# Right factors of the gated MLP in the projection's stream tiles, four of seven made inside the out projection; whole residual rows in two buffers; the first chunk's loads on ScalarE's queue

## The chip, the cores and the metric

One core of a Trainium2 chip runs the whole program in one launch. The metric is the device time in microseconds (us), the median of three runs. Engines are named as the profile names them: PE is TensorE's matmul and PEld its weight load, DVE is VectorE, ACT is ScalarE, POOL is GpSimd, SP is SyncE. A "q" behind a name (SPq, ACTq) is that engine's queue of transfers.

## What is computed

A trunk of two layers, one step for 1032 columns (1024 of a prompt, 8 of samples). Each layer has a mixer, then a gated MLP with a short convolution, both behind an RMSNorm and added to the stream:

```python
def _rmsnorm(x, g):
    y = xf * lax.rsqrt(jnp.mean(xf * xf, axis=-1, keepdims=True) + EPS)
    return (y * g.astype(jnp.float32)).astype(x.dtype)

def _conv_ffn(xn, w_up, conv_w, conv_b, w_down, conv_state):
    gpre, up = jnp.split(xn @ w_up, 2, axis=-1)
    full = jnp.concatenate([conv_state.astype(gpre.dtype), gpre], axis=1)
    acc = conv_b + full[:, 0:t] * conv_w[0]
    ...
    h = jax.nn.gelu(acc) * up
    return h @ w_down, full[:, full.shape[1] - (CONV_W - 1):]
...
        d, s_, c_, k_, w_ = _even_mixer(_rmsnorm(xs, norm_mix[l]), ...)   # ends in mixed @ w_out
        xs = xs + d
        ...
        d, cv = _conv_ffn(_rmsnorm(xs, norm_ffn[l]), *fp, state_ffn_conv[l])
        xs = xs + d
```

The model width is 1024 (8 blocks of 128 rows), the MLP's inner width 2816 (22 blocks, `NF`).

## The kernel before, in words

**Arithmetic.** Data lies transposed: 128 rows of a block on the partitions, TT = 1032 columns. A float32 product is made of three TensorE passes over a high and a low part of each operand: ACT writes the high part, DVE subtracts it from the value to get the low part. The stream of a layer is held as eight pairs `xh[m]`, `xl[m]`.

**Out projection** (`out_project`, L376 to L421). Eight output blocks m in the order `PAIRS` = 0, 4, 1, 5, 2, 6, 3, 7. Behind each block's matmuls (L285) POOL adds the block's high and low stream parts (L412), DVE adds the product (L416), ACT writes the new row times its gain to `big[:, m]` (L417), SP stores the row to `res` in DRAM (L418), ACT squares it (L419) and `add_sq` adds the squares up (L205).

**Climb** (`climb`, the up projection). The 1024 x 256 piece of the weight for one inner block f and the eight rows of `big` are cut into 2 x 2, and `seven` (L514) multiplies them by seven products instead of eight, in three PSUM banks in the order "abcabcb". A product has 24 matmuls of 258 columns (L534), 3 passes x 4 blocks x 2 halves. Its left factor comes from `factors` (L447): two loads of 512 KB into `wr` and `wr2` (L452), two sums on POOL (L456, L457), a split by ACT and DVE per product (L464, L466, L467). `fill` keeps four left factors ahead. Its right factor is four tiles (`slot`) of [128, 2, 2, 260]. There are 28 slots; they are made once, in f = 0, by `first` (L750), at the time when the product that needs them is issued: sums of `big` quarters (`sums`, L436 to L440) on POOL and DVE, then `parts`, a copy on ACT (L444) and a subtraction on DVE (L445). The pools of the out projection and of the stream tiles are closed by then, and the MLP's pools lie in their place. The inner blocks' results are turned into right factors of the next product and stored to `hid` in DRAM by SP (L718, L721, L722), through two staging tiles.

**Descend** (`descend`, the down projection). Pairs of inner blocks in chunks of two pairs, the last chunk of three; for each chunk four units j = 0 to 3, each of seven products of 12 matmuls (18 in the last chunk). Right factors come back from `hid` by `load_factors` (L602 to L607), the first chunk's on SP while the climb's last block still runs, later ones on ACT's queue. DVE (L810) adds each product to quarters of `big`. In chunks 1 and 2, behind product 6 of each unit, the residual of two half rows is loaded on SP (L826), multiplied by `std` (L827) and added to `big` (L828) on POOL; the halves share one tile `sq_t`.

**Layer 1's end.** Four inner blocks are left over. Behind the last chunk their rows `raw` are loaded (L584), split (`split_o`, L373, L374), and `finish` (L887) multiplies them by eight pieces of weight, which `last_weight` loads and splits (L260, L273, L274), then norms and transposes the output. At the end of layer 0, L595 and L596 split `big` into the stream tiles of layer 1.

**What sets the order.** Each engine runs its instructions in the order in which the program was written in the MLP (`ordered`); outside it a scheduler orders them. `plan(step, late, ...)` puts a piece of work behind the product with that number.

Of the kernel before, what the change touches and what calls it, by code (L numbers as in the profile page):

```python
# [9 lines left out]
F32 = mybir.dt.float32  # L10
# [61 lines left out]
class Trunk:  # L72
# [22 lines left out]
    def setup(self):  # L95
# [14 lines left out]
        self.order, self.rung = range(KD), 0  # L110
        self.open_x()
# [3 lines left out]
    def open_x(self):  # L115

        self.xp = self.tp(name="xp", bufs=1, side="right")
        pool = self.xp.__enter__()
        self.xh, self.xl = [None] * KD, [None] * KD
        for k in PAIRS[::-1]:  # L120
            self.xh[k], self.xl[k] = (pool.tile([128, TT], F32R, name=f"{x}{k}") for x in ("xh", "xl"))
# [255 lines left out]
    def out_project(self, l, w, split, ks, ready, late, nat=None):  # L377
# [3 lines left out]
        with self.tp(name="opp", bufs=2, space=PSUM) as pp, \  # L381
# [25 lines left out]
            self.res = self.dram.tile([KD, 128, TT], F32, name="res")  # L407
            for n, m in enumerate(PAIRS):
# [22 lines left out]
    def sums(self, i, b, eng):  # L431
# [9 lines left out]
        return self.halves((b11, b11, b21, b12, b11, b21, b22)[i])  # L441

# [105 lines left out]
    def ffn(self, l, last):  # L548
        nc, a, tc, big = self.nc, self.a, self.tc, self.big
        w_up, w_dn = a["ffn_w_up"][l], a["ffn_w_down"][l]  # L550
        pools = [self.tp(name="fr", bufs=1, side="right"), self.tp(name="fx", bufs=1, side="right"),
                 self.tp(name="fl", bufs=1)]
        self.fr, self.fx, self.fl = (p.__enter__() for p in pools)
        right = [self.slot(i) for i in range(8)] + [None] * 20
        for i in range(27, 7, -1):
            right[i] = self.slot(i)
        NP = 9 if last else 11
        hid = self.dram.tile([NP, 7, 128, 2, 2, QW + 2], F32, name="hid")
# [7 lines left out]
        self.st = self.fx.tile([128, 2, 2, QW + 2], F32R, name="st")  # L566
# [11 lines left out]
        pools.pop().__exit__(None, None, None)  # L578
        if last:
            with self.tp(name="fin", bufs=1) as fin:  # L580
                y = [fin.tile([128, TT], F32, name=f"y{i}") for i in range(4)]
                parts = []
                for k in range(4):
                    nc.sync.dma_start(y[k], raw[k])  # L584
                    parts.append(self.split_o(fin, k, y[k]))
                wts = [self.last_weight(w_dn[18 * 128:], 4, m, fin) for m in range(KD)]
                with self.tp(name="flp", bufs=8, space=PSUM) as self.ps:
                    self.finish(wts, [p[0] for p in parts], [p[1] for p in parts], y)
        while pools:
            pools.pop().__exit__(None, None, None)  # L590
        if not last:
# [1713 lines left out]
```

## Time and profile before

| | |
|---|---|
| median of three runs | 2974.23 us (2973.86 to 2976.27) |
| profiled execution | 2967.24 us; span of its records 2965.5 us |
| PE busy | 2753.7 us, 93% of the span |
| DVE, ACT, POOL busy | 61%, 45%, 38% |
| DMA, mean | 116 GB/s |
| mean granted TensorE clock | 0.96 of full speed |

The page also cuts the span into 40 equal slices of 74.1 us. Busy shares and the clock are in tenths:

```profile
PE   8999999999996999998878999999969999999798
...
PEclk9999999999897999999989999999979999999899
DMA  6620001531131344347755212221212344467522
```

A row of a timeline merges neighbours of one kind ("x22" is 22 instructions), and ends with the idle time of the engine ahead of it and what ended it. A row of the chain of waits is a piece of the path that ends last. Some matmul records are missing from the trace, so counts in the rows can be short of the program's.

### The profile page before, as it was taken

Reading aid. Unit: us, or ns where it says so; the run is one execution under the profiler, and the core shown is the slowest. Engines: PE = TensorE matmul, PEld = TensorE weight load, DVE = VectorE, ACT = ScalarE, POOL = GpSimd, SP = SyncE. Lnnn points to the kernel's source line nnn. Section 1 sums busy time; section 2 is a strip of 40 time slices with the busy share of each in tenths; the row PEclk is TensorE's granted clock in tenths of the full one; section 3 lists DMA queues with packets and bytes.
Section 4 is the critical chain, followed back from the end, with each engine's and each line's share of the span. In section 5 each row is a group of like instructions: output and inputs, shape, how many; then the busy total and the mean of one; then the engine's idle time right before and its main releaser. Section 6 shows DMA issues by size and latency. Waiting matters only on the chain.

```text
span 2965.5 us, 49527 instructions
## 1 busy us (share of the span) xinstructions
PE 2753.7 (93%) x19507; PEld 2496.5 (84%) x19507; DVE 1819.4 (61%) x3060; ACT 1334.1 (45%) x2543; POOL 1126.0 (38%) x1088
## 2 busy tenths in 40 slices
PE   8999999999996999998878999999969999999798
PEld 7885445887895999998878989888959999999698
DVE  6566765466626787776445754445356778765456
ACT  4343443334434666655434422324345666655234
POOL 3621234321153545553445411110344554554633
PEclk9999999999897999999989999999979999999899
DMA  6620001531131344347755212221212344467522
GB/s 182 187 63 29 36 1 56 192 108 37 42 96 31 103 151 157 138 139 271 247 172 200 55 36 66 63 63 45 89 50 65 139 149 151 142 224 260 194 83 108
DMA packets 300652, 342.67 MB, mean 116 GB/s; under 512 B 33997, under 2 KB 246068, under 8 KB 300356
## 3 DMA queue, kind: packets, MB, share of 16 engines
q1 hardware_dynamic: 269692, 238.97, 24.8%
q10 hardware_dynamic: 21000, 66.98, 6.2%
q0 software_dynamic: 9728, 33.56, 3.3%
q8 instruction: 154, 2.52, 0.4%
q14 instruction: 78, 0.64, 0.1%
HBM read 241.13 MB, written 102.50 MB: 116 GB/s over the span
## 4 chain that ended last, share of the span: by engine, by line
PE 78%; DVE 8%; POOL 4%; DMA 4%; ACT 3%; issue 2%; ACTq 0%; DVEq 0%; SPq 0%; POOLq 0%
PE ppb L534 16%; PE ps L285 13%; PE ppc L534 11%; PE ppa L534 10%; PE pp L285 6%; PE ps L1410 2%; PE pd L285 2%; DMA sq_t<-res 2%; PE ps L887 2%; PE pd L1319 1%; POOL big L828 1%; PE ps L1167 1%; PE pd L1385 1%; PE ps L1155 1%; PE pd L1386 1%
## 5 line engine op out<-in xcount | busy, mean ns | idle before, releaser
L534 PE MATMUL ppb<-s,wh 128*128 128x258 f32 x2376 | 315.8, 288 | 16.0 <-DVE s L445 5.3
L534 PE MATMUL ppb<-s,wl 128*128 128x258 f32 x2376 | 313.7, 287 | 9.6 <-ACT s L444 3.5
L534 PEld LDWEIGHTS ppb<-s,wh 128*128 128x128 f32 x2376 | 303.3, 196 | 18.2 <-ACT ps L466 6.2
L534 PEld LDWEIGHTS ppb<-s,wl 128*128 128x128 f32 x2376 | 300.4, 194 | 12.1 <-ACT s L444 4.1
L467 DVE TENSOR_TENSOR wh<-ps,wh 128x512 fp32r<-128x512 f32 (+2 forms) x280 | 162.4, 580 | 181.9 <-ACT ps L466 179.6
L534 PE MATMUL ppc<-s,wh 128*128 128x258 f32 x1536 | 211.5, 295 | 48.1 <-DVE big L810 22.8
L534 PE MATMUL ppc<-s,wl 128*128 128x258 f32 x1536 | 209.2, 292 | 47.5 <-DVE big L810 27.5
L534 PEld LDWEIGHTS ppc<-s,wh 128*128 128x128 f32 x1536 | 202.8, 202 | 50.2 <-ACT ps L466 18.0
L534 PEld LDWEIGHTS ppc<-s,wl 128*128 128x128 f32 x1536 | 199.6, 198 | 51.3 <-ACT wl L464 21.6
L467 DVE TENSOR_TENSOR wl<-ps,wl 128x512 fp32r<-128x512 f32 (+2 forms) x280 | 161.9, 578 | 131.0 <-ACT ps L466 129.3
L285 PE MATMUL ps<-xh,wh 128*128 128x344 f32 x960 | 223.7, 338 | 0.0
L285 PE MATMUL ps<-xl,wh 128*128 128x344 f32 x960 | 215.4, 328 | 5.1 <-DVE xl L596 2.7
L534 PE MATMUL ppa<-s,wl 128*128 128x258 f32 x1536 | 204.4, 287 | 14.1 <-ACT s L444 8.1
L272 POOL TENSOR_TENSOR wr<-wr,gains 128x1024 f32<-128x1024 f32 (+1 forms) x44 | 83.6, 1899 | 338.7 <-DMA wr<-in_odd_w_in_dram 217.0
L285 PE MATMUL ps<-xh,wl 128*128 128x344 f32 x960 | 210.6, 325 | 0.0
L534 PEld LDWEIGHTS ppa<-s,wl 128*128 128x128 f32 x1536 | 194.4, 194 | 17.0 <-ACT s L444 8.6
L534 PE MATMUL ppa<-s,wh 128*128 128x258 f32 x1536 | 200.8, 285 | 8.2 <-ACT tu L808 8.2
L534 PEld LDWEIGHTS ppa<-s,wh 128*128 128x128 f32 x1536 | 192.9, 192 | 8.9 <-ACT tu L808 8.4
L466 ACT COPY ps<-wr 128x512 f32<-128x512 f32 (+2 forms) x400 | 198.5, 496 | 2.8 <-DVE st L734 1.8
L464 ACT ACTIVATE wh<-wr 128x512 fp32r<-128x512 f32 (+2 forms) x200 | 108.6, 543 | 176.2 <-PE ppb L534 69.5
L464 ACT ACTIVATE wl<-wr 128x512 fp32r<-128x512 f32 (+2 forms) x200 | 108.6, 543 | 170.6 <-PE ppb L534 60.0
L472 POOL TENSOR_TENSOR wr<-wr,wr 128x512 f32<-128x512 f32 (+2 forms) x80 | 94.3, 1179 | 230.3 <-ACT ps L466 230.2
(780 smaller groups left out, 6064.4 us busy)
## 6 DMA issues: line engine op xcount, KB each, us to landing
s<-hid ACTq DMA_DIRECT2D x112, 520.0 KB
wr<-in_ffn_w_up_dram SPq DMA_DIRECT2D x88, 512.0 KB
hid<-big SPq DMA_DIRECT2D x67, 520.0 KB
hid<-st SPq DMA_DIRECT2D x66, 520.0 KB
wr<-in_ffn_w_down_dram SPq DMA_DIRECT2D x64, 256.0 KB
s<-hid SPq DMA_DIRECT2D x28, 520.0 KB
wr<-in_odd_w_in_dram SPq DMA_DIRECT2D x24, 512.0 KB
wr<-in_even_w_in_dram SPq DMA_DIRECT2D x18, 512.0 KB
```

Source lines behind the costliest of these rows:

```text
L272: self.gain_eng.tensor_tensor(raw, raw, gain[:, :, None].to_broadcast([128, kt, m]), op=OP.mult)
L285: nc.tensor.matmul(outs[g], l[:, kw, :], r[k][:, g * GW:(g + 1) * GW], start=(n == 0 and i == 0), stop=(n == kt - 1 and i == 2))
L464: nc.scalar.activation(hi, x, AF.Copy)
L466: nc.scalar.copy(pt, x)
L467: nc.vector.tensor_tensor(lo, pt, hi, op=OP.subtract)
L472: nc.gpsimd.tensor_tensor(a11, a11, a21, op=OP.subtract)
L534: nc.tensor.matmul(pt[:, q], w[:, k], r[:, part, q, :QW], start=(new and k == 0 and n == 0), stop=(k == len(right) - 1 and n == 2), skip_g ...
L828: p.tensor_tensor(big[:, m, s], big[:, m, s], x, op=OP.add)
L887: nc.tensor.matmul(pt, l[:, k, :], r[k][:, s], start=(k == 0 and i == 0), stop=(k == n - 1 and i == 2))
L1155: nc.tensor.transpose(pt[:, j * 128:(j + 1) * 128], kv[:, half * 4 + j, sl * 256 + c * 128:sl * 256 + c * 128 + 128], self.ident)
L1167: nc.tensor.matmul(hid[c][64 * h:64 * h + 64, :273], wt[:, c, q], xt[h][:, q, :273], start=(g == 0 and q == 0), stop=(g == 7 and q == 3))
L1410: nc.tensor.matmul(po[64 * g:64 * g + 64], v[:, kb, 64 * g:64 * g + 64], p[:, g * 512:(g + 1) * 512], start=first, stop=last)
```

## The change

1. The pool of the stream tiles stays open through the MLP. The 16 tiles `xh0` to `xl7` are slots 0 to 15; slots 16 to 27 are new tiles as before. A slot is [128, 2, 2, 258] now, so rows of `hid` have 4128 bytes instead of 4160, and the two zero fills of the pad are gone.
2. `prepare(j)` makes the right factors 0, 1, 2 and 4 of the column of blocks j, j + 4 (they are the ones that products 0 to 3 take) inside the out projection, behind every second block. All `sums` of `big` are on DVE. The twelve tiles of products 4 to 6 are planned three at a time behind products 0 to 3 of f = 0.
3. A residual row is loaded whole one unit ahead, at product 0, into `sq_t` or `sq` in turn; POOL multiplies at product 2 and adds at product 6. In layer 1 the eight rows are taken two units earlier.
4. The first chunk's loads are issued on ACT's queue.
5. At the end of layer 1 the four `raw` rows are loaded into free stream tiles, and the eight pieces of weight are loaded and split from m = 7 down to m = 0.
6. Layer 1's stream tiles come from the open pool.

```diff
+        self.pools.append(self.tp(name="xp", bufs=1, side="right"))
+        self.xp = self.pools[-1].__enter__()
         self.open_x()
...
+            self.right = [None] * 28
             for n, m in enumerate(PAIRS):
...
                 self.add_sq(x, n)
-        self.xp.__exit__(None, None, None)
+                if n % 2:
+                    self.prepare(n // 2)
...
     def slot(self, i):
-        return (self.fl if i > 7 else self.fr).tile([128, 2, 2, QW + 2], F32R, name=f"s{i}")
+        if i < 16:
+            return self.xp.tile([128, 2, 2, QW], F32R, name=("xh", "xl")[i // 4 % 2] + str(i % 4 + i // 8 * 4))
+        return self.fl.tile([128, 2, 2, QW], F32R, name=f"s{i}")
...
+    def quads(self, j):
+        return [self.big[:, m, s] for m in (j, j + 4) for s in (slice(0, HW), slice(HW, TT))]
+
+    def first_right(self, n, j):
+        i = 4 * MADE[n] + j
+        if i < 16:
+            self.right[i] = self.slot(i)
+        self.parts(self.right[i], self.halves(self.quads(j)[(0, 0, 2, 1, 0, 2, 3)[n]]))
+
+    def prepare(self, j):
+        for n in (0, 1, 2, 4):
+            self.sums(n, self.quads(j), self.nc.vector)
+            self.first_right(n, j)
...
-        pools = [self.tp(name="fr", bufs=1, side="right"), self.tp(name="fx", bufs=1, side="right"),
-                 self.tp(name="fl", bufs=1)]
+        pools = [self.tp(name="fx", bufs=1, side="right"), self.tp(name="fl", bufs=1)]
...
-                y = [fin.tile([128, TT], F32, name=f"y{i}") for i in range(4)]
-                parts = []
+                free = [self.slot(i).rearrange("p a q w -> p (a q w)") for i in (1, 3, 5, 7, 9, 11, 13)]
+                wts = [self.last_weight(w_dn[18 * 128:], 4, m, fin) for m in range(KD)[::-1]][::-1]
+                y, parts = [x.bitcast(F32) for x in free[:4]], free[4:]
+                while len(parts) < 8:
+                    parts.insert(3, fin.tile([128, TT], F32R, name=f"o{len(parts)}"))
                 for k in range(4):
                     nc.sync.dma_start(y[k], raw[k])
-                    parts.append(self.split_o(fin, k, y[k]))
-                wts = [self.last_weight(w_dn[18 * 128:], 4, m, fin) for m in range(KD)]
+                    nc.scalar.activation(parts[k], y[k], AF.Copy)
+                    nc.vector.tensor_tensor(parts[4 + k], y[k], parts[k], op=OP.subtract)
...
-        def first(i):
-            for n in ((0,), (1,), (2, 4), (3,), (), (6,), (5,))[i]:
-                for j in range(4):
-                    self.sums(n, xs[j], p if j < (2 if n == 1 else 3) else v)
-                for j in range(4):
-                    self.parts(right[4 * MADE[n] + j], self.halves(xs[j][(0, 0, 2, 1, 0, 2, 3)[n]]))
-            return right[4 * i:4 * i + 4]
+        for k in range(12):
+            self.plan(k // 3, 1, lambda k=k: self.first_right((3, 6, 5)[k // 4], k % 4))
...
-                        self.load_factors(c, n, hid, range(2 * i, min(2 * i + 2, 7)), nc.sync)
+                        self.load_factors(c, n, hid, range(2 * i, min(2 * i + 2, 7)), nc.scalar)
...
-                    for n in {1: (0, 1), 2: (2, 3)}.get(c, ()) if i == 6 else ():
-                        m, s = j + n // 2 * 4, slice(n % 2 * HW, n % 2 * HW + HW)
-                        x = self.vec.tile([128, TT], F32, name="sq_t")[:, s]
-                        nc.sync.dma_start(x, self.res[m][:, s])
-                        p.tensor_tensor(x, x, self.std[:, s], op=OP.mult)
-                        p.tensor_tensor(big[:, m, s], big[:, m, s], x, op=OP.add)
+                    r = 4 * c + j - (2 if last else 4)
+                    if i == 0 and -1 <= r < 7:
+                        rows[r + 1] = self.vec.tile([128, TT], F32, name=("sq_t", "sq")[r % 2])
+                        nc.sync.dma_start(rows[r + 1], self.res[r + 1])
+                    if i == 2 and 0 <= r < 8:
+                        p.tensor_tensor(rows[r], rows[r], self.std, op=OP.mult)
+                    if i == 6 and 0 <= r < 8:
+                        p.tensor_tensor(big[:, r], big[:, r], rows[r], op=OP.add)
```

**First place: SP's queue at the end of layer 0's out projection.** Before, the last stores of `res` and the MLP's first weight loads (`wr_7969` is the second half of f = 0's weights, a `wr2` tile):

```order
L418 DMA res<-rstd 128x1032
L452 DMA wr<-in_ffn_w_up_dram 128x8x128
L452 DMA wr_7969<-in_ffn_w_up_dram 128x8x128
L452 DMA wr_7977<-in_ffn_w_up_dram 128x8x128
L418 DMA res<-sq_t 128x1032
L418 DMA res<-rstd 128x1032
```

Now (`wr_8013` is that tile):

```order
L419 DMA res<-rstd 128x1032
L473 DMA wr<-in_ffn_w_up_dram 128x8x128
L419 DMA res<-sq_t 128x1032
L473 DMA wr_8013<-in_ffn_w_up_dram 128x8x128
L419 DMA res<-rstd 128x1032
L473 DMA wr_8021<-in_ffn_w_up_dram 128x8x128
```

The load of the second half went from ahead of the two last stores to between them. The pool `fx`, where it lands, now lies over the out projection's operands `oh` and `ol`, and the load waits for the last matmul of the out projection that reads them.

**Second place: POOL in the second chunk of layer 0, one unit.** Before, four residual operations on half rows (L827, L828) stand together between two operations of the left factors (L472, L476):

```order
L456 TENSOR_TENSOR s_14310<-wr_14205 128x256
L457 TENSOR_TENSOR s_14311<-s_14310,wr 128x256
L472 TENSOR_TENSOR wr<-wr,wr_14205 128x2x128
L827 TENSOR_TENSOR sq_t<-sq_t,std 128x516
L828 TENSOR_TENSOR big<-big,sq_t 128x516
L827 TENSOR_TENSOR sq_t<-sq_t,std 128x516
L828 TENSOR_TENSOR big<-big,sq_t 128x516
L476 TENSOR_TENSOR wr<-wr,s_14311 128x2x128
```

Now:

```order
L477 TENSOR_TENSOR s_14301<-wr_14194 128x256
L478 TENSOR_TENSOR s_14302<-s_14301,wr 128x256
L841 TENSOR_TENSOR sq<-sq,std 128x1032
L493 TENSOR_TENSOR wr<-wr,wr_14194 128x2x128
L843 TENSOR_TENSOR big<-big,sq 128x1032
L497 TENSOR_TENSOR wr<-wr,s_14302 128x2x128
```

Two operations on a whole row take the place of four, one of them ahead of the factor that was ahead of all four, and no transfer stands between them.

**Third place: ACT at the end of layer 1.** Before, behind the last left factor of the down projection (`fh` are high parts of `finish`'s weights, m = 0 first; `oh` those of the `raw` rows):

```order
L466 COPY ps<-wr_29104 128x384
L273 ACTIVATE fh_29592<-wr 128x512
L273 ACTIVATE fh_29598<-wr 128x512
L373 ACTIVATE oh_29571<-y_29566 128x1032
L373 ACTIVATE oh_29576<-y_29567 128x1032
L373 ACTIVATE oh_29581<-y_29568 128x1032
L373 ACTIVATE oh_29586<-y_29569 128x1032
L273 ACTIVATE fh_29604<-wr 128x512
```

Now (`fh_29489` is the piece for m = 7, `fh_29531` that for m = 0):

```order
L487 COPY ps<-wr_29017 128x384
L273 ACTIVATE fh_29489<-wr 128x512
L273 ACTIVATE fh_29495<-wr 128x512
L609 ACTIVATE o_29539<-xl_29483 128x1032
L273 ACTIVATE fh_29501<-wr 128x512
L273 ACTIVATE fh_29507<-wr 128x512
L273 ACTIVATE fh_29513<-wr 128x512
L273 ACTIVATE fh_29519<-wr 128x512
L273 ACTIVATE fh_29525<-wr 128x512
L273 ACTIVATE fh_29531<-wr 128x512
```

Three of the four splits of `raw` rows went ahead of the weights. All eight weights now stand ahead of the first matmul of `finish`, the one that it needs first at their end, and the tile of the first of them lies where the last chunk's last right factor is read.

## Rows read from the trace of the kernel before

**Rows 1.** The chain of work that ended last, its shares of the span by engine and then by line.

```profile
PE 78%; DVE 8%; POOL 4%; DMA 4%; ACT 3%; issue 2%; ACTq 0%; DVEq 0%; SPq 0%; POOLq 0%
PE ppb L534 16%; PE ps L285 13%; PE ppc L534 11%; PE ppa L534 10%; PE pp L285 6%; PE ps L1410 2%; PE pd L285 2%; DMA sq_t<-res 2%; PE ps L887 2%; PE pd L1319 1%; POOL big L828 1%; PE ps L1167 1%; PE pd L1385 1%; PE ps L1155 1%; PE pd L1386 1%
```

**Rows 2.** The timeline of TensorE around the start of the MLP of layer 0: start, duration (both us), engine, line, operation, tiles, shapes, count, and in brackets the idle time before it and what ended it. The first row is the out projection's last matmuls.

```profile
879.07 0.64 PE L285 MATMUL pp<-oh,wl 128*128 128x344 f32 x3
...
899.33 5.10 PE L534 MATMUL ppb<-s,wh 128*128 128x258 f32 x22 [2.65 <-DVE s L445]
...
911.04 0.80 PE L534 MATMUL ppc<-s,wl 128*128 128x258 f32 x2 [5.61 <-ACT s L444]
...
936.14 5.87 PE L534 MATMUL ppc<-s,wh 128*128 128x258 f32 x24 [7.33 <-ACT s L444]
...
944.54 2.91 PE L534 MATMUL ppb<-s,wl 128*128 128x258 f32 x22 [0.27 <-DVE s L445]
```

**Rows 3.** A stretch of that start by windows: length, busy time and count of each engine, granted TensorE clock, DMA share, GB/s.

```profile
890.00:900.00 10.00, 2.85 (x10) 2.11 (x10) 6.97 (x10) 3.95 (x7) 4.74 (x3) 0.50 0.00 1
```

**Rows 4.** The same timeline of TensorE for layer 1: the out projection's last matmuls and the last matmuls of the MLP's first seven products.

```profile
2167.13 0.62 PE L285 MATMUL pp<-oh,wl 128*128 128x344 f32 x3
...
2231.74 4.17 PE L534 MATMUL ppb<-s,wl 128*128 128x258 f32 x22 [0.27 <-DVE s L445]
```

**Rows 5.** The chain of waits at that start in layer 0, in order of time: start, duration, engine, tile, line.

```profile
897.97 0.70 DVE big L437
...
905.61 0.69 DVE wh L467
...
910.91 1.67 DVE big L439
...
921.49 1.01 PE ps L737 x2
922.50 2.87 PE ppa L534 x24
```

**Rows 6.** The timelines of VectorE, ScalarE and GpSimd late in the out projection of layer 0 (columns as in rows 2).

```profile
857.21 1.23 DVE L416 TENSOR_TENSOR rstd<-pp,rstd 128x1032 f32<-128x1032 f32 x1 [8.93 <-POOL sq_t L412]
...
870.18 0.63 ACT L464 ACTIVATE wh<-s 128x512 fp32r<-128x512 f32 x1 [0.61 <-POOL s L457]
...
868.85 1.29 POOL L457 TENSOR_TENSOR s<-s,wr 128x512 f32<-128x512 f32 x1
```

**Rows 7.** Windows of the down projection (columns as in rows 3): the first four chunks of layer 0, then the second and third chunk of layer 1.

```profile
1373.75:1437.63 63.88, 47.68 (x343) 46.53 (x342) 29.30 (x59) 35.45 (x88) 18.53 (x30) 0.87 0.83 294
1437.63:1488.51 50.88, 43.47 (x338) 42.95 (x337) 28.54 (x55) 19.29 (x57) 29.36 (x30) 0.93 0.64 220
1488.51:1554.93 66.42, 47.71 (x338) 46.84 (x337) 28.65 (x56) 18.40 (x56) 30.69 (x32) 0.85 0.52 177
1554.93:1605.17 50.24, 42.42 (x339) 42.20 (x337) 29.67 (x56) 19.75 (x56) 31.31 (x31) 0.93 0.68 230
...
2708.54:2754.70 46.16, 41.74 (x339) 40.70 (x338) 27.97 (x56) 19.13 (x57) 29.35 (x30) 1.00 0.69 243
2754.70:2826.00 71.30, 47.61 (x337) 46.74 (x336) 29.36 (x56) 19.19 (x56) 45.34 (x44) 0.81 0.58 202
```

**Rows 8.** The chain of waits in the second chunk of layer 0 (columns as in rows 5).

```profile
1460.68 6.95 DMA sq_t<-res
...
1467.77 1.27 POOL sq_t L827
...
1470.38 0.69 POOL wr L476
...
1472.99 2.92 PE ppc L534 x12
...
1480.04 1.44 PE ppb L534 x12
```

**Rows 9.** The chain of waits from the last columns of the up projection into the first chunk of layer 0 (columns as in rows 5).

```profile
1362.32 9.43 DMA hid<-big
...
1384.13 0.54 ACTq L606
```

**Rows 10.** The timeline of TensorE at the start of that chunk (columns as in rows 2).

```profile
1386.38 2.95 PE L534 MATMUL ppa<-s,wh 128*128 128x258 f32 x12 [8.16 <-ACT tu L808]
```

**Rows 11.** The timelines of TensorE, ScalarE and VectorE around the end of the last chunk of layer 1 (columns as in rows 2).

```profile
2893.24 2.31 PE L534 MATMUL ppb<-s,wh 128*128 128x258 f32 x18
2899.62 1.01 PE L887 MATMUL ps<-oh,fh 128*128 128x384 f32 x2 [4.07 <-ACT oh L373]
...
2888.66 0.63 ACT L273 ACTIVATE fh<-wr 128x512 fp32r<-128x512 f32 x1 [0.16 <-DMA wr<-in_ffn_w_down_dram]
2898.51 1.06 ACT L373 ACTIVATE oh<-y 128x1032 fp32r<-128x1032 f32 x1 [9.21 <-DMA y<-raw]
...
2897.41 1.29 DVE L274 TENSOR_TENSOR fl<-wr,fh 128x512 fp32r<-128x512 f32 x2
```

**Rows 12.** The chain of waits at the same place (columns as in rows 5).

```profile
2894.88 3.54 DMA y<-raw
```

**Rows 13.** The timeline of TensorE where layer 1 begins (columns as in rows 2).

```profile
1677.35 1.23 PE L285 MATMUL ps<-xl,wh 128*128 128x344 f32 x3 [2.67 <-DVE xl L596]
```

**Rows 14.** The instructions of line 1167: count, durations in ns (min/median/max), first and last start, shapes.

```profile
L1167 PE MATMUL ps<-xt,w x256: 391/393/444, 70.8 to 176.3; 128*64 128x273 f32 x128
```

More of the change, by code (lines that the diff above doesn't have):

```diff
@@ L115, in open_x @@
     def open_x(self):
-        self.xp = self.tp(name="xp", bufs=1, side="right")
-        pool = self.xp.__enter__()
         self.xh, self.xl = [None] * KD, [None] * KD
         for k in PAIRS[::-1]:
-            self.xh[k], self.xl[k] = (pool.tile([128, TT], F32R, name=f"{x}{k}") for x in ("xh", "xl"))
+            self.xh[k], self.xl[k] = (self.xp.tile([128, TT], F32R, name=f"{x}{k}") for x in ("xh", "xl"))
     def load_gains(self, tmp):
@@ L550, in ffn @@
         w_up, w_dn = a["ffn_w_up"][l], a["ffn_w_down"][l]
-        pools = [self.tp(name="fr", bufs=1, side="right"), self.tp(name="fx", bufs=1, side="right"),
-                 self.tp(name="fl", bufs=1)]
-        self.fr, self.fx, self.fl = (p.__enter__() for p in pools)
-        right = [self.slot(i) for i in range(8)] + [None] * 20
-        for i in range(27, 7, -1):
+        pools = [self.tp(name="fx", bufs=1, side="right"), self.tp(name="fl", bufs=1)]
+        self.fx, self.fl = (p.__enter__() for p in pools)
+        right = self.right
+        for i in range(27, 15, -1):
             right[i] = self.slot(i)
         NP = 9 if last else 11
-        hid = self.dram.tile([NP, 7, 128, 2, 2, QW + 2], F32, name="hid")
+        hid = self.dram.tile([NP, 7, 128, 2, 2, QW], F32, name="hid")
         raw = self.dram.tile([4, 128, TT], F32, name="raw")
@@ L577, in ffn @@
             assert not self.agenda
[L578 removed]
+        while pools:
+            pools.pop().__exit__(None, None, None)
         if last:
             with self.tp(name="fin", bufs=1) as fin:
[L581 to L582 removed]
+                free = [self.slot(i).rearrange("p a q w -> p (a q w)") for i in (1, 3, 5, 7, 9, 11, 13)]
[3 more added lines that the diff above has]
+                    parts.insert(3, fin.tile([128, TT], F32R, name=f"o{len(parts)}"))
                 for k in range(4):
                     nc.sync.dma_start(y[k], raw[k])
[L585 to L586 removed]
+                    nc.scalar.activation(parts[k], y[k], AF.Copy)
+                    nc.vector.tensor_tensor(parts[4 + k], y[k], parts[k], op=OP.subtract)
                 with self.tp(name="flp", bufs=8, space=PSUM) as self.ps:
[L588 to L591, printed above, removed]
+                    self.finish(wts, parts[:4], parts[4:], y)
+        else:
             self.open_x()
@@ L765, in after @@
                     for n, c in enumerate(chunks[0]):
-                        self.load_factors(c, n, hid, range(2 * i, min(2 * i + 2, 7)), nc.sync)
-            self.seven(pp, stream, first if f == 0 else lambda i: right[4 * i:4 * i + 4], after)
+                        self.load_factors(c, n, hid, range(2 * i, min(2 * i + 2, 7)), nc.scalar)
+            self.seven(pp, stream, lambda i: right[4 * i:4 * i + 4], after)
         self.plan(self.step + 3, 1, lambda: self.conv_store(l, cvp, cvs, rows))
@@ L776, in descend @@
         left, right = self.rstd[:, :HW], self.rstd[:, HW:]
-        squares, late = 0, deque()
+        squares, late, rows = 0, deque(), {}
         def scale():
```

7 lines of the change are left out of this document (2 added, 5 removed).

## The prediction

> **What bounds the kernel now.** I read the chain of waits first. 78% of the span is PE work, but 8% is DVE, 4% POOL and 4% DMA [rows 1], that is 16% or some 470 us in which PE waits; the loads of `sq_t` from `res` are the only transfers with a share of their own. So a gain must come out of stretches where PE stands, and I looked for them in PE's timeline. There are three kinds near this change.
>
> *The MLP's start.* The out projection ends at 879.71 (879.07 + 0.64), and the seven products of f = 0 end at 947.45 [rows 2]: 67.7 us. A product takes 2.87 us at full clock [rows 5], so seven need 20.1; norm sums between them take 1.01 at a time [rows 5]. Some 46 us are lost. The idle times name ACT L444 and DVE L445, the making of the right factors, and between the stalls the clock fell: 0.50 of full speed, the lower of its two levels (1.2 GHz), with PE busy 2.85 of 10 us [rows 3], so that 24 matmuls take 5.87 [rows 2]. Layer 1 shows the same: 2167.75 to 2235.91, 68.2 us [rows 4].
>
> *The residual in the down projection.* A product of 12 matmuls takes 1.44 [rows 8], so a chunk of 28 needs 40.3 us. Chunks 0 to 3 of layer 0 take 63.9, 50.9, 66.4 and 50.2 [rows 7]: 23.6, 10.6, 26.1 and 9.9 lost. In layer 1, chunk 1 loses 5.8 and chunk 2 31.0 [rows 7]. The chain of waits shows how: the transfer `sq_t<-res` takes 6.95, POOL stands behind it, then multiplies, adds and only then makes the left factor `wr` (L476), and PE resumes at 1472.99 at half clock, 2.92 for 12 matmuls [rows 8].
>
> *The first chunk of layer 0* waits for ACT and DVE that wait for stores of `hid`, one of them 9.43 from issue to landing [rows 9]; PE stands 8.16 [rows 10].
>
> **The change, part by part.** E is the end of the out projection.
>
> *Making right factors early.* `prepare` adds to each pair of blocks, on DVE, four sums and four subtractions, each 0.7 alone or 1.67 beside POOL [rows 5], so 5.6 to 13.4 us, and on ACT four copies at about 0.6 [rows 6]. In the out projection DVE stood 8.93 in one block [rows 6], 17.9 in a pair. That hides it; without that cover it would cost at most 13.4 a pair. I take nothing for the out projection. Behind E, product 0 has all its tiles, since the last (`xh3`) needs only the block before the last: it runs from E to E + 2.9.
>
> *The new wait.* The `wr2` half of f = 0's weights now waits for E on SP; the last store of `res` and the next weights queue behind it. A load of 516 KB lands 3.54 after issue [rows 12]; then POOL makes two sums of 1.29, ACT copies in 0.63 [rows 6], DVE splits in 0.69 [rows 5]: 7.4, or 6.8 for the first matmuls, which need only ACT's copy (with 0.04 of gaps and a shorter copy than that row's). So product 1 starts at E + 6.8 and PE stands 3.9, then runs it at half clock in some 5.4. Behind ACT's copy wait the last square and the copy of `xh7`, behind DVE's split the last sum of squares, so product 2 can lose some more. Then 5 x 2.87 and a norm sum of 1.0: 6.8 + 5.4 + 14.4 + 1.0 = 27.6. The twelve late tiles need 0.6 on ACT and 0.7 on DVE each, three behind a product of 2.87, so they keep pace, but beside left factors (two ACT operations a product) with little to spare; I add 2.4 for it: f = 0 ends at E + 30. **Gain 37.7 + 38.2 = 76 us.** Bounds: E + 25 (only the first stall) and E + 50 (each product also waits for its tiles, the seven making no better than half of the present way), 86 down to 36.
>
> *Residual.* The transfer now has a whole unit, 10.1 us, and 3 products more before POOL needs it, against 6.95. POOL's work is two operations on a whole row, each twice 1.27 [rows 8] or 2.5, and four of 0.7 for factors: 7.8 of 10.1. An add waits for DVE's last accumulation, some 1.5 behind the product, and holds up one factor by 2.5 more, against four factors made ahead, 4 x 1.44 = 5.8. In layer 1 two units also carry POOL's wide adds of the last chunk; I leave them a stall each. Of 10.6 + 26.1 + 9.9 = 46.6 I take back 40, of 36.8 in layer 1 32: **72 us**. Bounds: 36 (POOL's longer pieces stall half of the units) and 80.
>
> *Loads on ACT's queue.* The stores of `hid` are no longer behind loads in the same queue, but ACT issues 14 loads at 0.54 [rows 9] = 7.6 us and waits in order wherever a load waits for an earlier transfer. Of the first stall's 8.16 [rows 10] with its half clock I take back 8 in layer 0, and charge 1 in layer 1, which had nearly none. Bounds: 0 to 14, and -2 to +6. The stores were slow while the DMA engines were busy, 0.83 of the chunk [rows 7]. The Trainium skill ("DMA: Bandwidth & Descriptors", section "Issuing engines are not separate DMA queues") says that transfers of all issuing engines run on the same 16 DMA engines, so that another queue saves issue time only. By that rule this term would be 0 and the sum 8 less; it is rival 1.
>
> *The end.* The `raw` rows come early, which saves their 3.54 [rows 12] and most of the split. But the eight weights now all come ahead of `finish`'s first matmul, m = 0 last, and the first of them waits for the last product. There are two `wr` tiles, so after two splits come three more rounds of two pieces: a transfer of 256 KB (2.7, as 516 KB took 3.54), ACT 0.63, DVE 0.65 [rows 11], 4.0 in all, beside 1.25-us splits of `raw` rows. 0.6 + 0.7 + 3 x 4.0 + 2 = 15.5 us after 2894.9 against the 4.7 of now (2899.62) [rows 11]. **Loss 11 us**, 7 to 14. Nothing later gives it back, since all that follows comes out of `finish`'s matmuls.
>
> *Layer 1's stream tiles*: three pairs are split before the last product ends; the present 2.67 [rows 13] shrinks, gain 2 (0 to 4). The pad's 32 bytes: nothing, see rival 4.
>
> **Sum**: -76 - 72 - 8 + 1 + 11 - 2 = -146. The profiled execution took 2967.24, so 2821; the median of the runs was 7.0 above it (2974.23), so **2828 us**.
>
> **Rivals.** *1, the queue does not matter*: the stores are slow because the DMA engines are full, and ACT's waits for transfers cost the 6 of the bound: 8 + 6 more, 2842. For it speaks the DMA share of 0.83 [rows 7]; against it, that a store which now stands behind loads in its own queue should land sooner once they have left it. *2, the MLP's start stays a chain*: the late `wr2` and ACT's and DVE's backlog make each product wait; f = 0 ends at E + 48, 36 more, 2864. For: ACT L444 and DVE L445 end nearly every wait there now [rows 2]; against: 16 of 28 tiles are ready at E. *3, POOL holds the factors*: 36 of the 72 stay, 2864. For: POOL is busy 45 of 71 us in layer 1's chunk 2 [rows 7]; against: the chain passes through the transfer each time. *4, slower*: the right factors' rows of 258 columns without pad start at multiples of 1032 bytes, so half of the matmuls of the MLP read from an address that is no multiple of 16, where all were before. There are 10,896 of them at 120 ns (2.87/24 [rows 5]); if reading cost each 13.4 ns more, the 146 are gone, and at 20 ns the time is 3046. Line 1167 speaks against it: its rows of 274 columns start at multiples of 1096 bytes, half off 16 too, yet its 256 matmuls lie at 391 to 393 from least to median [rows 14]; but it computes in plain float32.
>
> **How the numbers follow.** Forecast 0.48, rival 1 0.20, rival 2 0.14, rival 3 0.13, rival 4 0.05. The best bounds of the start, the residual, the loads and the end together are 86 + 80 + 16 - 7 + 4 = 179, 2795; it is unlikely that all hold, so I begin at 2798. Rivals 2 and 3 end at 2864, which is the upper end; both at once and rival 4 lie outside. 0.2% of this kernel, 6 us, is about what a measurement can tell from no change; only rival 4, with a price between, comes near: faster 0.95, same 0.01, slower 0.04.
>
> **What would show it.** Right: in the profile after, PE stands about 4 us behind the first product of f = 0 and ends it near E + 30; no `sq_t<-res` in the chain; chunks 1 and 2 near 42 us; PE idle 15 us before `finish`. Wrong: a product of 24 matmuls that takes over 2.95 at full clock (rival 4), idle times ended by ACT or DVE all through f = 0 (2), by POOL's L841 or L843 (3), stores of `hid` still near 9 us (1). If chunks lose their time to loads of `hid` once the residual is out of the way, my 72 is too high.

## The result: 2864.9 us, 109 less than before, 37 more than predicted

The changed kernel takes 2864.94 us (median of 4 runs, 2856.33 to 2872.85), the kernel before beside it 2974.05 (2968.68 to 2976.27). The ratio is 0.9635, 95% interval 0.9601 to 0.9669: clearly faster, and 0.94 us above the upper end of the range. The profiled execution took 2869.35, its span 2867.6; between the two profiled spans lie 97.9 us.

The chain of waits after, shares of the span by engine and by line, to be held against [rows 1]:

```profile
PE 82%; DVE 7%; DMA 3%; ACT 3%; issue 2%; POOL 2%; ACTq 0%; SPq 0%; DVEq 0%; POOLq 0%
PE ppb L555 18%; PE ps L285 14%; PE ppa L555 11%; PE ppc L555 11%; PE pp L285 6%; PE ps L1425 2%; PE pd L285 2%; PE ps L902 2%; PE pd L1334 1%; PE ps L1182 1%; PE pd L1400 1%; PE ps L1170 1%; PE pd L1401 1%; PE ps L1580 1%; DMA wr<-in_ffn_w_down_dram 1%
```

PE rose from 78% to 82%, POOL fell from 4% to 2%, and the residual's transfer is gone. To see where the time went I cut both traces at the first matmul of each stage: all 10,896 product matmuls are in every trace (a row that counts fewer than 24 or 12 is a piece of a product), so a stage ends where the next one's count begins. "f0" is from the out projection's end to the second block, "end" all behind the last product. "To E" is the stretch up to the out projection's end E, "last" a layer's last chunk. Columns: before, changed, and five experiments (us).

```
            before  changed  x1_sp  x3_wr2  x4_res  x5_tail  x10_best
L0 to E      879.7   883.2   904.3   915.2   909.3   882.4    901.9
L0 f0         67.9    37.8    37.8    33.8    67.9    37.5     33.7
L0 f1         23.2    23.7    23.7    23.7    23.2    25.5     23.7
L0 f2-20     382.8   384.3   384.3   384.3   382.8   384.3    384.3
L0 f21        20.2    27.6    20.2    27.8    20.2    28.4     20.2
L0 chunk 0    63.9    61.6    65.2    60.9    66.5    60.4     67.0
L0 chunk 1    50.9    40.5    40.5    40.5    40.3    40.5     40.5
L0 chunk 2    66.4    40.4    40.4    40.4    40.3    40.4     40.4
L0 chunk 3    50.2    40.4    40.4    40.4    40.4    40.4     40.4
L0 last       69.0    69.9    69.9    71.3    69.0    69.9     71.0
L1 to E      493.5   496.9   492.6   494.3   491.9   495.3    492.4
L1 f0         68.6    36.9    37.1    33.4    67.9    36.8     33.7
L1 f1         24.4    25.6    23.8    24.5    23.2    25.6     24.2
L1 f2-20     382.8   384.3   384.3   384.3   382.8   384.3    384.3
L1 f21        20.2    25.3    20.2    25.7    20.2    25.9     20.2
L1 chunk 0    44.8    48.7    47.8    48.3    50.0    49.4     47.9
L1 chunk 1    46.1    40.4    40.4    40.4    40.3    40.5     40.4
L1 chunk 2    71.7    41.6    41.6    41.5    41.3    41.5     41.4
L1 last       69.2    77.2    76.3    77.2    69.0    69.5     69.5
end           69.9    81.3    80.8    81.0    69.9    70.2     69.6
```

The residual's chunks fell to their floor. f = 0 fell by 61.9 in both layers together. But other stages grew: f21 by 12.6 and f2 to f20 by 3.0 in both layers together, the last chunk of layer 1 by 8.0, the end by 11.4, and layer 1's first chunk by 3.9 where layer 0's fell by 2.3.

**The MLP's start**, PE's timeline of the changed kernel, to be held against [rows 2]. E is 883.17.

```profile
883.01 3.02 PE L555 MATMUL ppa<-xh,wl 128*128 128x258 f32 x24
891.97 5.88 PE L555 MATMUL ppb<-xl,wh 128*128 128x258 f32 x24 [5.94 <-ACT wh L485]
...
913.64 3.12 PE L555 MATMUL ppb<-s,wl 128*128 128x258 f32 x24
920.25 0.41 PE L860 MATMUL ps<-ident,sq 88*128 88x88 f32 x1 [3.50 <-DVE wl L488]
920.95 5.16 PE L555 MATMUL ppa<-xh,wh 128*128 128x258 f32 x24
```

Most of the stalls are gone. Product 0 runs at once, the predicted stand follows it, 5.94 where 3.9 was expected, and half clock behind it (granted clock 0.50, the lower level of 1.2 GHz; 5.88 for 24). A second stand of 3.50 comes behind the seventh product; the clock was 0.50 from 920.95 to 923.5, and the next 24 took 5.16. The chain of waits names both:

```profile
883.20 4.58 DMA wr<-in_ffn_w_up_dram
...
887.92 1.66 POOL s L477
...
889.66 1.61 POOL s L478
...
891.29 0.63 ACT wh L485
...
913.95 1.06 ACT std L759
915.02 1.28 ACT L235
916.32 1.07 ACT rstd L237
...
918.38 0.61 ACT wl L485
```

First the `wr2` load that waits for E, 4.58 (3.54 was taken) and the two POOL sums at 1.66 and 1.61 (1.29 was taken); a sum on DVE ran beside them until 890.14. Then the norm on ACT: 4.4 us pass from its start (L759) to the split of a left factor (L485).

**The last block of the climb**, ACT's timeline and the transfers in the chain of layer 0, then PE:

```profile
1337.73 7.27 ACTq L628 DMA_DIRECT2D xh<-hid  x4
...
1345.05 0.63 ACT L485 ACTIVATE wh<-wr 128x512 fp32r<-128x512 f32 x1 [7.10 <-DMA xl<-hid]
...
1359.28 0.64 ACT L738 ACTIVATE st<-big 128x516 fp32r<-128x516 f32 x1 [6.67 <-DMA hid<-st]
```

```profile
1337.73 12.40 DMA xh<-hid
1350.19 8.98 DMA hid<-st
...
1360.68 5.22 DMA hid<-st
```

```profile
1352.07 4.71 PE L555 MATMUL ppb<-s,wh 128*128 128x258 f32 x24 [5.60 <-ACT big L738]
```

Four issues of loads hold ACT from 1337.73 for 7.27 us, since an earlier load has to land before the next is issued. The trace's semaphores say which. Every transfer that SP or ACT issues reports its landing on one of the same eight semaphores in turn, and each issue here waits until the transfer that had its semaphore before has landed: in this row the issue at 1340.85 follows a landing at 1340.78, those at 1342.65 and 1344.68 landings at 1342.62 and 1344.60. So a wait can be for a transfer of the other engine's queue: the store of `hid` that SP issued at 1350.19 had its data at 1348.10, and came behind the load that ACT issued at 1337.73 and that landed at 1350.13. Transfers that POOL issues have eight semaphores of their own.

The split of a left factor (L485), the copies and the staging of `hid` stand behind ACT's issues. And the store still takes 8.98, hardly less than the 9.43 before [rows 9]; a later one takes 5.22. This is what rival 1 expected.

**The last chunk and the end of layer 1**, the chain of waits, ACT and PE:

```profile
2703.47 11.00 DMA xl<-raw
...
2714.55 0.33 ACTq L628
```

```profile
2714.98 0.52 ACT L485 ACTIVATE wl<-s 128x384 fp32r<-128x384 f32 x1 [5.94 <-DMA xl<-raw]
```

```profile
2717.13 2.95 PE L555 MATMUL ppb<-xl,wl 128*128 128x258 f32 x12 [5.74 <-DVE big L823]
...
2802.53 0.69 PE L902 MATMUL ps<-xh,fh 128*128 128x384 f32 x1 [16.27 <-ACT fh L273]
```

The issue of one of the last chunk's loads on ACT, at 2714.55, waits for a `raw` row that SP issued and that landed at 2714.48: the two have one semaphore. ACT stands 5.94 at it, and PE stands 5.74 for what follows. The 16.27 ahead of `finish` was expected (15.5).

**Where layer 1 begins**, PE before and, in the second block, now. The stand of 2.67 [rows 13] has become 0.25 and two more under 1 us, and the transposes that come next wait longer for DVE, which has the norm ahead of `sq`:

```profile
1701.27 0.44 PE L2129 MATMUL ps<-ident,sq 128*128 128x128 f32 x2 [1.13 <-DVE sq L336]
```

```profile
1611.46 0.75 PE L285 MATMUL ps<-xl,wh 128*128 128x344 f32 x3 [0.25 <-DVE xl L618]
...
1636.10 0.69 PE L2144 MATMUL ps<-ident,sq 128*128 128x128 f32 x2 [4.13 <-DVE sq L336]
```

### The profile page after: what moved, and what is told of

The parts are those of the page before. It is cut to its first block, busy times and chain, and to the rows that moved or that the text cites. A ratio compares the mean times of both kernels' runs of the same rounds, so it can differ in the third digit from the quotient of the medians.

```text
span 2867.6 us, 49399 instructions
## 1 busy us (share of the span) xinstructions
PE 2729.6 (95%) x19507; PEld 2480.6 (87%) x19507; DVE 1846.7 (64%) x3080; ACT 1338.2 (47%) x2543; POOL 1093.7 (38%) x1025
## 4 chain that ended last, share of the span: by engine, by line
PE 82%; DVE 7%; DMA 3%; ACT 3%; issue 2%; POOL 2%; ACTq 0%; SPq 0%; DVEq 0%; POOLq 0%
PE ppb L555 18%; PE ps L285 14%; PE ppa L555 11%; PE ppc L555 11%; PE pp L285 6%; PE ps L1425 2%; PE pd L285 2%; PE ps L902 2%; PE pd L1334 1%; PE ps L1182 1%; PE pd L1400 1%; PE ps L1170 1%; PE pd L1401 1%; PE ps L1580 1%; DMA wr<-in_ffn_w_down_dram 1%
## 5 line engine op out<-in xcount | busy, mean ns | idle before, releaser
L555 PE MATMUL ppb<-s,wh 128*128 128x258 f32 x1380 | 183.5, 288 | 12.1 <-DVE sq L682 6.5
L555 PEld LDWEIGHTS ppb<-s,wh 128*128 128x128 f32 x1380 | 176.4, 195 | 12.8 <-ACT big L738 5.8
L555 PE MATMUL ppb<-s,wl 128*128 128x258 f32 x1380 | 179.2, 284 | 0.5 <-DVE sq_t L682 0.4
L285 PEld LDWEIGHTS ps<-xl,wh 128*128 128x128 f32 x960 | 164.9, 192 | 10.3 <-issue 4.5
L555 PEld LDWEIGHTS ppb<-s,wl 128*128 128x128 f32 x1380 | 171.9, 190 | 1.3 <-issue 0.9
L485 ACT ACTIVATE wh<-wr 128x512 fp32r<-128x512 f32 (+2 forms) x200 | 108.7, 544 | 135.7 <-PE ppb L555 54.6
L285 PEld LDWEIGHTS ps<-xh,wh 128*128 128x128 f32 x960 | 163.0, 192 | 6.5 <-issue 3.3
L285 PEld LDWEIGHTS ps<-xh,wl 128*128 128x128 f32 x960 | 164.7, 192 | 3.0 <-issue 2.6
L485 ACT ACTIVATE wl<-wr 128x512 fp32r<-128x512 f32 (+2 forms) x200 | 108.8, 544 | 123.5 <-PE ppb L555 55.6
L700 DVE SCALAR_TENSOR_TENSOR big<-big 128x524 f32<-128x524 f32 x176 | 130.6, 780 | 9.3 <-ACT big L697 9.2
L497 POOL TENSOR_TENSOR wr<-wr,s 128x512 f32<-128x512 f32 (+2 forms) x80 | 86.6, 1082 | 94.1 <-ACT ps L487 94.1
L1341 DVE TENSOR_REDUCE m<-pd 128x1 f32<-128x512 f32 (+3 forms) x130 | 83.1, 661 | 49.4 <-PE pd L1339 38.6
```

The costliest lines, as they stand in the source:

```text
L285: nc.tensor.matmul(outs[g], l[:, kw, :], r[k][:, g * GW:(g + 1) * GW], start=(n == 0 and i == 0), stop=(n == kt - 1 and i == 2))
L485: nc.scalar.activation(hi, x, AF.Copy)
L497: nc.gpsimd.tensor_tensor(a12, a12, s2, op=OP.subtract)
L555: nc.tensor.matmul(pt[:, q], w[:, k], r[:, part, q, :QW], start=(new and k == 0 and n == 0), stop=(k == len(right) - 1 and n == 2), skip_g ...
L700: v.scalar_tensor_tensor(cv[:, c], g[:, n + c.start:n + c.stop], taps[:, 22 * n + f:22 * n + f + 1], cv[:, c], op0=OP.mult, op1=OP.add)
L1341: nc.vector.tensor_reduce(m2[:, n, g, i0:i0 + hs, br], pt, AX.X, OP.max)
```

## The experiments

Two theories stood. **Mine**: three terms of the sum were mis-sized, for reasons of their own: ACT as an issuer pays with its compute (f21, last chunk), the start has a later first factor and the norm, and the early `raw` rows cost. **The rival**: PE's new stands come from full DMA engines and busy ACT and DVE whatever the queue or place, so that no single edit gives them back. The kernel before had medians of 2972 to 2991 us in these comparisons, so I compare ratios to the kernel before on the same chip, and stages. The stretch up to E took 878 to 915 us, and 879.7, 909.3 and 878.9 in three kernels in which it is the same code (before, x4_res, x7_unpad). It goes mostly with the chip: 904 to 915 in four kernels on one, 878 to 882 in four on a second, 902 and 904 on a third (the chip of the first comparison isn't on record). Where nothing near them was changed, most stages behind repeat within some tenths, f1, f21, the first chunks and the stretch up to layer 1's E within 2 to 5 us.

**x1_sp**, the loads back on SP:

```diff
-                        self.load_factors(c, n, hid, range(2 * i, min(2 * i + 2, 7)), nc.scalar)
+                        self.load_factors(c, n, hid, range(2 * i, min(2 * i + 2, 7)), nc.sync)
```

> Only the first chunk's loads go back to SP's queue. Theory A (ScalarE, which issues in order, stands until an earlier transfer has landed, and its copies and splits stand behind it): the last block of the up projection goes from 27.6 and 25.3 us back to 20.2 in both layers, the first chunk from 61.6 to about 64 in layer 0 and from 48.7 to about 45 in layer 1; in all about 14 us less than the changed kernel. Rival B (the DMA engines are full there and any queue waits): the last block keeps its 5 to 7 us and the time stays within 3 us of the changed kernel. Rival C (stores stand behind loads in one queue, as the prediction had it): the first chunk grows by 8 us and more and the time is not shorter.

Ratio 0.9617 (0.9600 to 0.9634). f21 is 20.2 in both layers, as theory A says; chunk 0 is 65.2 and 47.8. Together 9.7 less than the changed kernel (12.4 from f21, -3.6 and +0.9 from the chunks, the 0.9 within that stage's spread) where 14 was expected, since layer 1's first chunk hardly fell. Whole time alone would not show it, the two intervals overlap; the stages do. B is out for f21. The 8 us of C did not come, and its mechanism falls with the next one.

**x11_poolq**, the same loads on POOL's queue (`nc.gpsimd`):

> The first chunk's loads are issued on GpSimd's queue, so they stand neither on ScalarE nor ahead of the stores on SP. Theory A (ScalarE's waits as issuer cost the last block, and a queue without stores serves the stores): the last block takes 20.2 us and the first chunk of layer 0 under 60, of layer 1 under 46. Rival B (the DMA engines are full, so a queue of its own does not serve the stores): last block 20.2, first chunks as with SP, 65 and 48. Rival C (GpSimd in turn stands as issuer and its sums for the last block and for the left factors are late): the last block keeps 3 us and more.

Ratio 0.9615 (0.9594 to 0.9637). f21 20.2 and 20.2, chunk 0 67.0 and 49.5. Its chain of waits:

```profile
1360.09 12.37 DMA hid<-big
...
1374.60 8.62 DMA hid<-big
```

Neither ACT nor the stores' own queue holds the loads now, they share no semaphore with the stores, and the stores take 12.37 and 8.62 from issue to landing. So B: what delays the stores is not their place in a queue. The rule of the Trainium skill that the prediction weighed ("DMA: Bandwidth & Descriptors", "Issuing engines are not separate DMA queues") is what the runs show: 8.98 beside loads on ACT, 12.37 and 8.62 beside loads on POOL.

**x2_fin**, the order of the last weights alone:

```diff
-                wts = [self.last_weight(w_dn[18 * 128:], 4, m, fin) for m in range(KD)[::-1]][::-1]
+                wts = [self.last_weight(w_dn[18 * 128:], 4, m, fin) for m in range(KD)]
```

> Only the order of the eight last weights is turned back to m = 0 first; the raw rows still come early. Theory A (the order alone makes TensorE stand 16.3 us before the last stage): the stand falls to 5 us or less and the kernel is about 11 us shorter than the changed one. Rival (what counts is that the first split waits for the last product, and that all splits share two raw buffers): the stand stays over 12 us.

Ratio 0.9600 (0.9578 to 0.9621). The end falls from 81.3 to 67.5, 2.4 under before, and PE goes into `finish` without a stand:

```profile
2801.93 0.87 PE L555 MATMUL ppb<-xl,wh 128*128 128x258 f32 x6
2802.82 0.44 PE L902 MATMUL ps<-xh,fh 128*128 128x384 f32 x1
```

The order makes the 16.27. The last chunk keeps its 77.4.

**x5_tail**, the same order, and the `raw` rows in tiles over the last chunk's right factors:

```diff
+                y = [fin.tile([128, TT], F32, name=f"y{i}") for i in range(4)]
                 free = [self.slot(i).rearrange("p a q w -> p (a q w)") for i in (1, 3, 5, 7, 9, 11, 13)]
-                wts = [self.last_weight(w_dn[18 * 128:], 4, m, fin) for m in range(KD)[::-1]][::-1]
-                y, parts = [x.bitcast(F32) for x in free[:4]], free[4:]
+                wts = [self.last_weight(w_dn[18 * 128:], 4, m, fin) for m in range(KD)]
+                parts = list(free)
```

> The end of layer 1 put back: the raw rows land in tiles that lie where the last chunk's right factors are, so that they load behind it, and the last weights are built from m = 0 up. Theory A (the early raw rows take the DMA engines and ScalarE's place in its own queue of loads while the last chunk's tiles load): the last chunk of layer 1 goes from 77.2 us back to 69.9, the last stage from 81.3 to 70; 18 us less than the changed kernel. Rival (the last chunk's stand comes from the loads on ScalarE's queue alone or from the residual's places): the last chunk stays at 77 and only 11 us go.

Ratio 0.9543 (0.9524 to 0.9561). Last chunk 69.5, end 70.2: 18.8 less. Theory A's times hold, and the 8 us of the last chunk belong to the early `raw` rows (x2_fin, with the rows still early, keeps them); x4_res says the same from the other side. Only its "own queue of loads" is off: the `raw` rows were in SP's queue, and held ACT by the shared semaphore shown above.

**x3_wr2**, `wr2`, `s1` and `s2` at the start of the pool `fl`, over an operand of the out projection that is read early in its last block:

```diff
-        nc, ext = self.nc, self.fx
+        nc, ext = self.nc, self.fl
...
+        for _ in range(2):
+            for name in ("s1", "s2"):
+                self.fl.tile([128, 4, 128], F32, name=name, bufs=1)
+            self.fl.tile([128, KD, 128], F32, name="wr2", bufs=2)
         for i in range(27, 15, -1):
             right[i] = self.slot(i)
...
```

> Only the places of the tiles wr2, s1 and s2 change: they lie where the out projection's operand that is read early lies, so the second half of the first weights loads before the out projection ends. Theory A (the late load costs the first stand of 5.9 us and the half clock behind it): the first block of the up projection goes from 37.8 and 36.9 us to about 29 in each layer, 16 us in all. Rival B (ScalarE and VectorE are behind with tiles and splits anyway): product 1 starts early but products 2 to 4 wait instead, and the block stays over 34 us.

Ratio 0.9610 (0.9594 to 0.9627). f0 is 33.8 and 33.4, under B's 34, far from A's 29. PE's timeline (E is at 915.2):

```profile
919.80 0.75 PE L555 MATMUL ppb<-xl,wh 128*128 128x258 f32 x4 [1.73 <-ACT wh L485]
921.89 2.69 PE L555 MATMUL ppb<-xl,wh 128*128 128x258 f32 x20 [1.34 <-DVE wh L488]
...
948.27 0.41 PE L860 MATMUL ps<-ident,sq 88*128 88x88 f32 x1 [3.49 <-DVE wl L488]
```

The late load was worth 3.7 us a layer. Behind it ACT and DVE are late with the last block's row and tiles: the split of product 1's factor stands behind them in order. The 3.49 behind product 6 is untouched.

**x6_conv**, `conv_setup` two products later. With this edit the first block's convolution reads its coefficients before they are written, so it does not wait for them either; the instructions and their sizes are the same.

```diff
-                self.conv_setup(taps, sts, sums["rows"])
+                self.plan(self.step + 2, 1, lambda: self.conv_setup(taps, sts, sums["rows"]))
```

> conv_setup, four transposes on TensorE that wait for a PSUM bank of the left factors, is put two products later. Theory A (TensorE stands 3.5 us at the start of f = 1 for that bank, since ScalarE works at the norm, 4.5 us, before it splits the next left factor, while product 0's own factors are ready): the stretch of f = 0 goes from 37.8 and 36.9 to about 34 and 33.4, f = 1 stays under 24. Rival B (the left factors themselves are late behind the norm): the stand moves into f = 1, which grows by what f = 0 loses.

f0 fell by 4.3 and 4.1 (33.4 and 32.8), and f1 grew by 4.8 and 4.5 (28.6 and 30.1); ratio 0.9623 (0.9607 to 0.9639). PE now stands for DVE in f = 1, and for the same bank later:

```profile
916.70 3.14 PE L555 MATMUL ppb<-xl,wl 128*128 128x258 f32 x24 [2.50 <-DVE sq_t L688]
922.22 0.29 PE L860 MATMUL ps<-ident,sq 88*128 88x88 f32 x1 [2.37 <-DVE wh L488]
```

My theory fell, B held: the bank was only where the lateness showed.

**x4_res**, the kernel before with the residual part alone (the last hunk of the diff, and the dictionary `rows` that it fills):

> The kernel before with the residual part alone: whole rows in two buffers, loaded one unit ahead, in layer 1 two units earlier. Theory A (the transfer of a residual row was what held GpSimd and so the left factors): chunks 1 to 3 of layer 0 take 40.4 us each, chunks 1 and 2 of layer 1 40 to 42, 82 us less than before in all, if the stand at the last chunk of layer 1 (77.2 against 69.2 in the changed kernel) belongs to the early raw rows and not to this part; 74 if it belongs to this part. Rival (part of the gain came with the other parts, such as shorter rows): under 60 us.

Ratio 0.9747 (0.9726 to 0.9768), 75 us. Chunks 1 to 3 of layer 0 fell by 46.5, chunks 1 and 2 of layer 1 by 36.2: 82.7, the whole loss. The first chunks grew by 2.7 and 5.1, and the last chunk of layer 1 stayed at 69.0. So this part alone is some seven tenths of the gain (2.5% of 3.65%). What went is POOL's wait for the transfer: before, POOL waits for `sq_t<-res` 17 times, 75.2 us in all; here and in the changed kernel it has no such wait. Loading early and whole rows were not tested apart.

**x7_unpad**, the kernel before without the pad (each `QW + 2` is `QW`, the stage's `+ 8` and the zero fills are gone):

> The kernel before with the pad of the right factors taken out and nothing else. Theory A (rows that start off a multiple of 16 bytes cost a product matmul 0.46 ns): the spacing of the products' matmuls goes from 119.9 to 120.4 ns, the blocks f = 2 to 20 from 382.8 to 384.3 us, 5 us in all. Rival (the changed kernel's longer spacing comes from its busier engines or from other places of the tiles): 119.9 and 382.8 stay.

The mean spacing of the product matmuls of f2 to f20, from start to start, is 119.9 ns before and 120.4 here and in the changed kernel. f2 to f20 take 384.4 in each layer against 382.8. Theory A's numbers hold: 10,896 x 0.5 ns = 5 to 6 us. The time lies where theory A puts it: of each pair of matmuls the second reads the half of the columns whose rows start off 16 bytes without the pad, and the time from its start to the next one's rose from 120.6 to 122.1 ns, while that behind the first went from 119.3 to 118.8. The whole, a ratio of 1.0001 (0.9987 to 1.0014), does not show it, as other stages were shorter in that run (layer 1's chunk 0 by 1.8).

**x8_all**, x1_sp, x3_wr2, x5_tail and x6_conv's edits together (so its first block's convolution, too, reads its coefficients early):

> The changed kernel with four corrections at once: the first chunk's loads on SP, the early places of wr2, s1 and s2, conv_setup two products later, the end of layer 1 put back. If the terms add up: f = 0 at about 30 us in each layer, the last block of the up projection at 20.2, the first chunk at 65 and 48, the last chunk of layer 1 at 69.9, the last stage at 70: about 43 us less than the changed kernel, a ratio to the kernel before of 0.949. Rival (the stands of f = 0 take each other's place): over 0.953.

Ratio 0.9506 (0.9489 to 0.9523), between the two. f0 29.4 and 29.4, f1 30.1 and 28.6: what x6_conv's edit took from f0 it gave to f1 (x10_best, without it, has 33.7 and 23.7 in layer 0).

**x10_best**, the same without x6_conv's edit:

> The changed kernel with three corrections whose stages were measured one by one: the first chunk's loads on SP, the early places of wr2, s1 and s2, the end of layer 1 put back. If the terms add: last block of the up projection 12.5 us less, first chunks 2.7 more, f = 0 7.4 less, last chunk of layer 1 7.7 less, last stage 11.1 less: 36 us less than the changed kernel, a ratio to the kernel before of 0.951. Rival (the corrections take each other's gain, since with early weights the loads on SP meet the residual's): over 0.955.

Ratio 0.9521 (0.9506 to 0.9535): 2848.93 us against 2991.37 beside it. The three corrections add up (last column of the table): without the two stretches up to E it takes 35 us less than the changed kernel, 36 were expected. This version beats both kernels: its interval lies below that of the changed one, and two of its parts simply undo parts of the change. By whole times alone it can't be told from x5_tail, whose interval overlaps.

## Why the prediction was wrong, point by point

The direction and most places were right, the sum was 48 us too high in the profiled spans (146 against 98) and 37 in the medians (146 against 109).

- **Making right factors early**: right in kind, and no out projection is longer for it (its matmuls span 98.6 and 97.2 us before, 98.5 and 97.2 now, and product 0 starts at E). Of 76 us, 61.9 came. The step that failed is "f = 0 ends at E + 30": its seventh product ended at 916.76, E + 33.6, and the 3.5 behind it was not foreseen. Two parts of it are seen in the trace. The first factor came at E + 8.8, not E + 6.8, as the load took 4.58 and POOL's sums 1.66 and 1.61. And the norm's 4.4 us on ACT, hidden before inside a chain that was later still, now stand in front of f = 1's left factors. x3_wr2 took 3.7 a layer off the first, and x6_conv only moved the second, so no single wait holds the rest. That ACT and DVE are the bound from E to f = 1, as rival 2 said (at less than half its price, 14 of 36), fits this; no run relieved them.
- **Residual**: 72 forecast, 82.7 in the chunks, 75 with what the first chunks lost to it (x4_res). The step was right: the chunks went to a floor of 40.3 to 41.6, so POOL's longer pieces stalled next to nothing.
- **Loads on ACT's queue**: -7 forecast, +9.7 measured (changed kernel against x1_sp). The step that failed is its premise, that stores wait behind loads of their own queue. A store took 8.98 with the loads on ACT's queue and 12.37 with them on POOL's. The cost was known to the text, ACT's waits in order, but was priced at 6 at most and only in layer 1: it was 7.4 in layer 0's f21 and 5.1 in layer 1's. That the waits are for the transfers of both queues was not seen. This is rival 1, and I gave it 0.20.
- **The end**: 11 forecast, 11.4 measured, and for the reason given (x2_fin). The terms of that sum add up to 15.3, not 15.5, which leaves the loss at 11. But the early `raw` rows were booked as a saving, and cost 8 in the last chunk: their transfers came where the last chunk's loads were being issued. The text had no term for it.
- **The pad**: "nothing" was 5 us by the spacing of all product matmuls, 3.0 of it in f2 to f20 (x7_unpad): rival 4's mechanism at 0.5 ns, not 13.4. Line 1167, in plain float32, had not shown it, as the text feared.
- **Layer 1's stream tiles**: 2 forecast. The stand of 2.67 went, but the norm behind it took the time back: the in projection's 72nd matmul ends 15.3 to 15.8 us behind the last product with the change and 18.0 to 18.9 without, the 96th 30.9 to 34.7 and 32.6 to 35.3. The step that failed is taking the shorter stand for a gain. The whole stretch up to layer 1's E takes 492.1 to 496.9 with the change and 491.7 to 493.5 without.
- The stretch up to layer 0's E is 3.5 longer, which is less than it varies by with the same code.

Stage by stage, measured less forecast in the two profiled spans: the start 14.1, f21 and the first chunks 21.2 (forecast -7, measured +14.2), layer 1's last chunk 8.0, the stretch up to layer 1's E 5.4, f2 to f20 3.0, the end 0.4, the other stages 6.0, less 9.9 by which the residual's chunks fell more than 72: 48 in all. Of the 14.2, x1_sp gives 9.7 to the loads; the residual's part alone made the first chunks 7.8 longer (x4_res), and by their spread these two need not add up. That the time lies 0.9 us from the price of rivals 2 and 3 is chance: neither came as written. The range ended at 2864 because its upper end came from one rival alone; several parts that each fail a little were left outside with "both at once".

## What to carry to other kernels

An engine that computes and also issues transfers waited here, in order, for earlier transfers before it could issue the next, and for those of another engine's queue too where both report on the same semaphores. In a stretch where the DMA engines are busy, price such an issue by the landing time of the transfers ahead and ask what compute stands behind it. Another queue did not make a transfer land sooner there. When a stall is taken out of a chain, look for the next engine that was late behind it: here the norm on ScalarE came out where the tile making had covered it, and moving the instruction at which it showed only moved the stand; where layer 1 begins, VectorE's norm took back what the stream tiles had gained.

## What the runs showed of the hardware that was not expected

- The pace of float32r matmuls of 258 columns went with where the rows of the moving operand start: 119.9 ns with starts at multiples of 16 bytes (before, x4_res), 120.4 with half of them at 8 off (x7_unpad, the changed kernel), and the added time lies behind the matmuls of that half. Other offsets were not tried.
- In the chains of waits around the first chunk, stores of half a megabyte took 8.98 and 5.22 us beside loads on ACT's queue, 8.98 beside loads on SP's (x1_sp) and 12.37 and 8.62 beside loads on POOL's.
- Transfers issued by SP and ACT report on the same eight semaphores in turn, so that an issue on one engine can wait for a landing on the other's queue (1350.19 behind 1350.13, 2714.55 behind 2714.48).
- The stretch up to layer 0's E took 879.7, 909.3 and 878.9 us in three kernels that have the same code there, far more spread than in any stage behind it. It goes mostly with the chip (904 to 915, 878 to 882, 902 and 904 us on three of them). What differs between the chips isn't shown.
